# Spreading norms by whole-array transposes, padding the low parts to 128 rows, and shifting dense work into the pairs of a delta-rule layer

## The chip, the cores and the metric

The kernel runs on one core of one Trainium2 chip. The metric is the device time of one launch in microseconds (us). The engines are TensorE (PE, matmuls; its weight loads are listed as PEld), VectorE (DVE), ScalarE (ACT), GpSimd (POOL) and SyncE (SP, which here only issues DMAs).

## The reference

A trunk of two residual layers over 512 tokens of width 1024, in float32: a spatial-gating MLP, a gated convolutional feed-forward layer, an RWKV-7 time-mixing layer and a second feed-forward layer, each behind an RMS norm. All edits lie in the time-mixing layer (16 heads of width 64):

```python
xx = token_shift(h) - h
xr, xw, xk, xv, xa, xg = (h + xx * mu[i] for i in range(6))
r, k, v = xr @ w_r, xk @ w_k, xv @ w_v
w = -softplus(-(w0 + tanh(xw @ w1) @ w2)) - 0.5
a = sigmoid(a0 + (xa @ a1) @ a2)
g = sigmoid(xg @ g1) @ g2
kk = heads(k * k_k)
kk = kk * rsqrt(maximum(sum(kk * kk, -1), 1e-24))     # norm over the 64 of a head
k = k * (1 + (a - 1) * k_a)
decay = exp(-exp(heads(w)))
# S_t = S_{t-1} diag(decay_t) + (S_{t-1} (-kk_t)) (kk_t a_t)^T + v_t k_t^T ;  y_t = S_t r_t
y = group_norm(wkv7_scan(...)) * ln_w + ln_b + sum(r * k * r_k, -1) * v
out = (y * g) @ w_o
```

## The kernel before, in words

Activations are kept transposed, features on the 128 partitions and the 512 tokens along the free dimension, as eight tiles of 128 features. Each large product is made of three matmuls of fp32r operands (`mm3`): every float32 operand is split into a rounded high part and a low part, and high x high, high x low and low x high are added up in PSUM. A *dense step* below is the work between two yields of `dense_steps`: two of the eight contraction tiles, six matmuls 128x128 by 512.

The recurrence is computed in chunks of 64 tokens. `rwkv_first` makes the low-rank products `r.lr` and the receptance. `rwkv_main` then runs these generators against each other:

- `pairs()` is the main work of the first part. It goes over eight pairs of heads. `decay(p)` (three yields) applies the second factors of the two low-rank products (`l2`, two column blocks loaded at a time by `second_factors`), takes tanh, a running sum over tokens and exponentials, and computes the norm of each key over its head: squares (L884), sums by head with tokens on the partitions (L894, eight columns), a reciprocal (L897), and a spread of these reciprocals back to features by tokens (L902, eight matmuls with an identity into `u.q`, each of two instructions and 64 output rows). `operands(p)` multiplies them into the keys (L922). `products(p)` (three yields) forms the within-chunk products and stores them to DRAM for the scan.
- `projections()` is the *fill*: eight key tiles, eight value tiles, then the gate's product (`gates`) and the output projection (`project`). The mixed inputs of the values, `r.mix(3, k)`, one ACT and one DVE operation and a split into high and low parts, are issued while the last two key tiles are multiplied. High and low parts share two rings of ten buffers (`mxh`, `mxl`), eight of which hold the key inputs until then. `value(m)` centres a value tile (L839), stores it for the scan, and later adds the bonus of its pair (L854, L856). `gate_mix` makes the mixed inputs of the gate.
- `invert(g)` is the *side* work: the inverses of the triangular blocks of four pairs, 31 short dependent steps of two DVE operations and then small matmuls.
- `scan(g)` goes over the eight chunks of a group of four pairs in order, three yields each; `finish` normalises the result of every two chunks.

`weave(main, side, fill, rate, lag, side_rate)` interleaves them: after each yield of the main work, `rate` is added to a due count, and for each whole unit one step of the fill is issued; its PE instructions are queued behind a recent PE instruction of the main work. `RATES` holds the rates of six stages: pairs up to the fourth, pairs beside the first inverse, first scan (beside the second inverse), second scan, the scan's last normalisation, and the last pair. What is left of the fill comes after the second scan. Within these rules a planner orders each engine's instructions; the engines then run them in that order.

The low part of the second factors is one tile, `l2[2]`, whose lower 64 rows belong to the decay and whose upper 64 rows to the in-context rate; each matmul with it contracts 64 rows (L872).

Of the kernel before, what the change touches and what calls it, by code (L numbers as in the profile page):

```python
# [12 lines left out]
F32 = mybir.dt.float32  # L13
F32R = mybir.dt.float32r
AF = mybir.ActivationFunctionType
ALU = mybir.AluOpType
# [4 lines left out]
P = 128  # L21
D = 1024
KT = 8
T = 512
NF = 22
C = 64
# [3 lines left out]
GN_EPS = 64e-5  # L30
C1 = -0.5 * math.exp(-0.5)

RATES = ((1.9, 2), (1.9, 6, 2.2), (0.66, 2, 1.15), (0.72, 2), (2, 2), (1.2, 6, 2.2))
LEAD = 1
WB = 4
FIRST0, WAIT, STEPS = 1, 1, (2, 2, 2, 2, 2)
# [108 lines left out]
class Emit:  # L145
# [596 lines left out]
    def rwkv_main(self, r, ctx, gain):  # L742
        nc, tc, A = self.nc, self.tc, self.A
        V, S, G = nc.vector, nc.scalar, nc.gpsimd
        h0, h1 = slice(0, 64), slice(64, 128)
        H = (h0, h1)
# [4 lines left out]
        ep = ctx.enter_context(tc.tile_pool(name="pairs", bufs=1))  # L751

        def tile_(shape, tag, bufs):
            return ep.tile(shape, F32, tag=tag, bufs=bufs, name=self.uid(tag))

        def tmp(tag, bufs, w=W2):
            return tile_([P, w], tag, bufs)

        def c3(t):
            return t.rearrange("p (c t) -> p c t", t=C)  # L760

        def bc(t, n):
            return t.unsqueeze(2).to_broadcast([t.shape[0], t.shape[1], n])

        ks, used, done, vdone = {}, set(), set(), set()
        l2 = []
# [3 lines left out]
        def second_factors(p):  # L770

            w32 = self.l2w.pop()
            l2[:] = [ep.tile([P, 2 * P], F32R, tag=f"l2{i}", bufs=1, name=self.uid("l2")) for i in range(3)]
            for j in range(2):
                w = w32[:, 512 * j:512 * j + 2 * P]
                S.copy(l2[j], w)
                V.tensor_tensor(l2[2][H[j]], w[H[j]], l2[j][H[j]].bitcast(F32), ALU.subtract)
            if p + 2 < KT:
                self.load_l2(p + 2)


        def projections():

            load = Ahead([lambda n=n, m=m: self.parts(n, m) for n in PARTS for m in range(KT)])

            def key(m, a):
                while m >= NKEY and m - NKEY not in used:
                    yield
                ks[m] = tmp("key", NKEY, T)
                S.copy(ks[m], a)  # L790

            for m in range(KT - 2):
                a = self.acc("mm")
                yield from self.dense_steps(a, load.take(), r.xk)
                yield from key(m, a)
                yield

            ws = [load.take(), load.take(False)]
            accs = [self.acc("mm") for _ in range(2)]
            xv = []  # L800
            for k in range(KT):
                for j in range(2):
                    self.mm3(accs[j], self.wcols(ws[j], k * P, P), r.xk[k], k == 0, k == KT - 1)
                while len(xv) < min(k + 3, KT):
                    xv.append(r.mix(3, len(xv)))
                if k == 4:
                    load.fetch()
                yield
            for j in range(2):
                yield from key(KT - 2 + j, accs[j])  # L810
            late = iter(())
            for m in range(KT):
                a = self.acc("mm")
                w = load.take()
                if m == KT - 2:
                    ga["w"] = load_gate(0)
                for n, _ in enumerate(self.dense_steps(a, w, xv)):
                    yield
                    next(late, None)
                    if m == KT - 1 and n == 0:  # L820
                        gw[0] = gate_weights(ga["w"])
                        ga["parts"] = self.gate_parts()
                    if m == KT - 1 and len(gx) < 2:
                        gx.append(gate_mix(len(gx)))
                for _ in late:
                    yield
                v = ip.tile([P, T], F32, tag="v", bufs=1, name=self.uid("v"))
                S.copy(v, a)
                late = value(m, v)
            next(late)  # L830
            tail.append(late)
# [30 lines left out]
        def scratch(tag):  # L862
            return self.gp.tile([P, T], F32, tag=tag, bufs=2 if tag == "sq" else 1, name=self.uid(tag))

        def decay(p, u):

            k, w = ks[p], slice(p % 2 * P, (p % 2 + 1) * P)
            accs = [self.acc("e") for _ in range(2)]
            for j in range(2):
                nc.tensor.matmul(accs[j], l2[j][:, w], r.lr[j], start=True, stop=False)  # L870
            for j in range(2):
                nc.tensor.matmul(accs[j], l2[2][H[j], w], r.lr[j][H[j]], start=False, stop=True)  # L872
            if p % 2 == 1 and p + 1 < KT:
                second_factors(p + 1)
            th, u.ta = scratch("sq"), tmp("ta", 2, T)
            for j, x in enumerate((th, u.ta)):
                S.activation(x, accs[j], AF.Tanh, scale=0.5, bias=dq(j, p))
            u.kn = tmp("kn", 2, T)
            S.activation(u.kn, k, AF.Copy, scale=dq(2, p))
            V.tensor_scalar(th, th, 1.0, None, ALU.add)  # L880
            yield
            V.tensor_tensor_scan(th, self.c("smask", T), th, 0.0, ALU.mult, ALU.add)
            sq = scratch("sq")
            S.activation(sq, u.kn, AF.Square)  # L884
            u.gt = tile_([P, NCH, C + 1], "gt", 1)
            G.memset(u.gt[:, :, 0:1], 1.0)
            S.activation(u.gt[:, :, 1:], c3(th), AF.Exp, scale=C1)
            S.activation(gc[:, p], c3(th)[:, :, C - 1], AF.Exp, scale=C1)
            u.ei = scratch("rb")
            S.activation(u.ei, th, AF.Exp, scale=-C1)  # L890

            q = self.acc("e")
            for b in range(4):
                nc.tensor.matmul(q[:, 2 * b:2 * b + 2], sq[:, b * P:(b + 1) * P], self.c("blk2", 2), start=True, stop=True)  # L894
            n2 = tile_([P, 8], "n2", 2)
            V.tensor_scalar(n2, q[:, 0:8], 1e-24, None, ALU.max)
            V.reciprocal(n2, n2)  # L897
            yield
            u.q = self.acc("e")
            for b in range(4):  # L900
                for hd in range(2):
                    nc.tensor.matmul(u.q[H[hd], b * P:(b + 1) * P], n2[:, 2 * b + hd:2 * b + hd + 1].to_broadcast([P, C]),  # L902
                                     self.c("ident", P), start=True, stop=True)
            yield

        def operands(p, u):
# [152 lines left out]
        def gate_mix(k):  # L1059
            with ExitStack() as behind:  # L1060
                for eng in (mybir.EngineType.DVE, mybir.EngineType.Activation):
                    behind.enter_context(tc.issue_after(self.last(eng)))
                j, t = 5 * KT + k, scratch("sq")
                S.activation(t, self.hz[k][:, 0:T], AF.Copy, scale=self.p("mu", j))
                V.scalar_tensor_tensor(t, self.h[k], self.omu[:, j:j + 1], t, ALU.mult, ALU.add)
                return self.operand(t)
# [56 lines left out]
        def load_gate(g):  # L1123
            cols = slice(512 * g, 512 * g + 512)
            w32 = self.wp.tile([P, 1024], F32, tag="w32", bufs=2, name=self.uid("w32"))
            self.wq.dma_start(w32[:, 0:512], A["g2"][0:P, cols])
            self.wq.dma_start(w32[0:32, 512:], A["g2"][P:P + 32, cols])
            return w32

        def gate_weights(w32):  # L1130
            ws = ep.tile([P, 512], F32R, tag="gw", bufs=1, name=self.uid("gw"))
            self.stack(ws, w32[0:32, 512:], False)
            return (*self.split(ep, w32[:, 0:512], [P, 512], "gw", bufs=1), ws)
# [186 lines left out]
        main = pairs()  # L1320
        self.weave(until(main, lambda: 3 in done), None, fill, *RATES[0], ktiles=STEPS[0])
        inv = invert(0)
        for _ in take(inv, FIRST0):
            pass
        self.weave(until(main, lambda: KT - 2 in done), inv, fill, *RATES[1], ktiles=STEPS[1])
        load(0, 0)
        self.weave(main, inv, fill, *RATES[5], ktiles=STEPS[1])
        ahead = invert(1)
# [4 lines left out]
        ep = ctx.enter_context(tc.tile_pool(name="scan", bufs=1))  # L1333
        inv = ahead
        r.sg = [ep.tile([P, T], F32R, name=f"sg{i}") for i in range(3)]
        for _ in range(LEAD):
            next(fill, None)
        self.weave(scan(0), inv, fill, *RATES[2], ktiles=STEPS[2])
        for _ in inv:
            pass  # L1340
        self.weave(scan(1, left.pop()), None, fill, *RATES[3], ktiles=STEPS[3])
        self.weave(left.pop(), None, fill, *RATES[4], ktiles=STEPS[4])
        for _ in fill:
# [71 lines left out]
```

## Time and profile before

| | |
|---|---|
| three runs | 1256.67, 1258.59, 1263.21 us (median 1258.59) |
| profiled execution | 1258.64 us, of which 1256.8 us from its first to its last instruction |
| granted clock of PE, mean | 0.998 |
| spatial-gating layer | about 0 to 157 us of the span |
| first feed-forward layer | about 157 to 516 us |
| time mixing: first products | about 516 to 574 us |
| time mixing: pairs | about 574 to 731 us |
| time mixing: first and second scan | about 731 to 847 us |
| time mixing: rest of the projection | about 847 to 890 us |
| second feed-forward layer and output | about 890 to 1257 us |

A row of the timeline reads: start in us, duration in us, engine, line of the kernel, operation, written tile <- read tiles, shape, count. A shape such as 64*128 ahead of the operand's says how much of the array a matmul uses, rows by columns. Matmul durations overlap, because they are pipelined and their ends are modelled. A row of the busy-time view reads: stretch of the span, its length, then busy us and count of instructions of each engine, the clock that PE was granted, the mean share of time that the DMA engines were busy, and GB/s.

### The profile page before, as it was taken

Reading aid. Unit: us, or ns where it says so; the run is one execution under the profiler, and the core shown is the slowest. Engines: PE = TensorE matmul, PEld = TensorE weight load, DVE = VectorE, ACT = ScalarE, POOL = GpSimd, SP = SyncE. Lnnn points to the kernel's source line nnn. Section 1 sums busy time; section 2 is a strip of 40 time slices with the busy share of each in tenths; the row PEclk is TensorE's granted clock in tenths of the full one; section 3 lists DMA queues with packets and bytes.
Section 4 is the critical chain, followed back from the end, with each engine's and each line's share of the span. In section 5 each row is a group of like instructions: output and inputs, shape, how many; then the busy total and the mean of one; then the engine's idle time right before and its main releaser. Section 6 shows DMA issues by size and latency. Waiting matters only on the chain.

```text
span 1256.8 us, 19427 instructions
## 1 busy us (share of the span) xinstructions
PE 1238.0 (98%) x7543; PEld 1003.2 (80%) x7543; DVE 856.3 (68%) x1403; ACT 627.7 (50%) x1080; POOL 95.0 (8%) x117
## 2 busy tenths in 40 slices
PE   9999999999999999999999999899999999999997
PEld 6878888888888888877777777677888888888886
DVE  6466568888886454775798898775677787773233
ACT  6444446555554333475676657533544454442322
POOL 4100200000000010000000022322100000000000
PEclk9999999999999999999999999999999999999999
DMA  7332457777656775325777799784323332333332
GB/s 260 103 101 84 130 170 243 244 248 246 205 165 204 219 218 191 108 87 191 218 200 215 217 242 219 205 205 135 93 92 101 101 99 88 99 96 93 105 96 80
DMA packets 115452, 201.65 MB, mean 160 GB/s; under 512 B 21600, under 2 KB 53600, under 8 KB 115360
## 3 DMA queue, kind: packets, MB, share of 16 engines
q10 hardware_dynamic: 39104, 112.87, 29.7%
q1 hardware_dynamic: 76256, 87.54, 23.6%
q8 instruction: 59, 0.97, 0.3%
q14 instruction: 33, 0.27, 0.1%
HBM read 152.93 MB, written 47.45 MB: 159 GB/s over the span
## 4 chain that ended last, share of the span: by engine, by line
PE 86%; DVE 7%; issue 1%; POOL 1%; ACT 0%; DMA 0%; DVEq 0%; POOLq 0%; ACTq 0%
PE mm L320 9%; PE mm L322 9%; PE mm L321 9%; PE aux L320 6%; PE aux L322 6%; PE aux L321 6%; PE e L320 6%; PE e L321 6%; PE us L320 6%; PE e L322 6%; PE us L322 6%; PE us L321 6%; DVE tt L1022 1%; PE aux L945 1%; DVE pr L1021 1%
## 5 line engine op out<-in xcount | busy, mean ns | idle before, releaser
L236 ACT CAST w<-w 128x512 fp32r<-128x512 f32 x340 | 205.9, 611 | 349.1 <-PE aux L322 88.5
L237 DVE TENSOR_TENSOR w<-w,w 128x512 fp32r<-128x512 f32 x340 | 232.5, 686 | 181.4 <-ACT w L236 180.9
L320 PE MATMUL mm<-mxh,w 128*128 128x512 f32 x416 | 170.0, 409 | 0.2 <-ACT vt L844 0.2
L321 PE MATMUL mm<-mxl,w 128*128 128x512 f32 x416 | 164.3, 395 | 0.0
L322 PE MATMUL mm<-mxh,w 128*128 128x512 f32 x416 | 164.2, 395 | 0.0
L347 POOL TENSOR_TENSOR ss<-ss,sq 128x512 f32<-128x512 f32 x30 | 40.8, 1362 | 768.8 <-ACT sq L345 706.1
L320 PEld LDWEIGHTS mm<-mxh,w 128*128 128x128 f32 x416 | 78.2, 188 | 20.2 <-issue 3.3
L322 PEld LDWEIGHTS mm<-mxh,w 128*128 128x128 f32 x416 | 78.4, 188 | 16.7 <-issue 0.7
L321 PEld LDWEIGHTS mm<-mxl,w 128*128 128x128 f32 x416 | 78.4, 188 | 15.6 <-issue 1.3
L549 ACT ACTIVATE cv<-z,par 128x512 f32<-128x512 f32 x88 | 71.7, 816 | 33.5 <-DVE z L547 28.7
L320 PE MATMUL aux<-mxh,w 128*128 128x512 f32 x216 | 84.5, 391 | 0.0
L320 PE MATMUL us<-mxh,w 128*128 128x512 f32 x216 | 84.5, 391 | 0.0
L322 PE MATMUL aux<-mxh,w 128*128 128x512 f32 x216 | 84.2, 390 | 0.0
L321 PE MATMUL us<-mxl,w 128*128 128x512 f32 x216 | 84.1, 389 | 0.0
L321 PE MATMUL aux<-mxl,w 128*128 128x512 f32 x216 | 84.1, 389 | 0.0
L322 PE MATMUL us<-mxh,w 128*128 128x512 f32 x216 | 84.0, 389 | 0.0
L320 PE MATMUL e<-mxh,w 128*128 128x512 f32 x208 | 81.4, 391 | 0.0
L321 PE MATMUL e<-mxl,w 128*128 128x512 f32 x208 | 81.2, 390 | 0.0
L322 PE MATMUL e<-mxh,w 128*128 128x512 f32 x208 | 81.0, 389 | 0.0
L550 DVE SCALAR_TENSOR_TENSOR cv<-z,par,cv 128x512 f32<-128x512 f32 x88 | 66.0, 751 | 19.5 <-ACT cv L549 19.5
L551 DVE SCALAR_TENSOR_TENSOR cv<-z,par,cv 128x512 f32<-128x512 f32 x88 | 66.0, 751 | 2.9
L237 DVE TENSOR_TENSOR pwl<-pw,pwh 128x512 fp32r<-128x512 f32 (+1 forms) x51 | 34.8, 682 | 19.8 <-DMA wkd<-pwl 4.6
(1081 smaller groups left out, 2559.8 us busy)
## 6 DMA issues: line engine op xcount, KB each, us to landing
w<-in_wup ACTq DMA_DIRECT2D x88, 512.0 KB, 3.6
w<-in_wdn ACTq DMA_DIRECT2D x32, 512.0 KB, 3.6
st<-std SPq DMA_DIRECT2D x30, 320.0 KB, 6.8
w<-wkd ACTq DMA_DIRECT2D x16, 512.0 KB, 4.5
w<-wvd ACTq DMA_DIRECT2D x16, 512.0 KB, 5.5
w<-wod ACTq DMA_DIRECT2D x16, 512.0 KB, 4.2
w<-in_wdn ACTq DMA_DIRECT2D x16, 384.0 KB, 3.3
w<-in_wsu ACTq DMA_DIRECT2D x8, 512.0 KB, 3.8
```

Of the source, the lines that this page charges most:

```text
L236: nc.scalar.copy(hi[r, :n], src)
L237: (lo_eng or nc.vector).tensor_tensor(lo[r, :n], src, hi[r, :n].bitcast(F32), ALU.subtract)
L320: mm(acc, wh, xh, start=first, stop=False)
L321: mm(acc, wh, xl, start=False, stop=False)
L322: mm(acc, wl, xh, start=False, stop=last)
L347: nc.gpsimd.tensor_tensor(self.ss, self.ss, self.sq, ALU.add)
L549: nc.scalar.activation(c, z[:, 2:], AF.Identity, scale=cw(2, i), bias=self.p("conv_b", l * 44 + i))
L550: nc.vector.scalar_tensor_tensor(c, z[:, 1:T + 1], cw(1, i), c, ALU.mult, ALU.add)
L551: nc.vector.scalar_tensor_tensor(c, z[:, 0:T], cw(0, i), c, ALU.mult, ALU.add)
L945: nc.tensor.matmul(qs[hd][:, c - ch.start, :], bk[H[hd], c, C * hd:C * hd + P], ar[H[hd], c, :], start=True, stop=True)
L1021: V.tensor_tensor(q, a, b, ALU.mult)
L1022: V.tensor_tensor(tt[:, 0:nj, j + 1:32], tt[:, 0:nj, j + 1:32], q, ALU.add)
```

## The change

Four edits. The reciprocals of the norms are first copied by ACT into a 128x512 array in which each stands 64 times, and four whole-array transposes then take the place of the eight half-wide matmuls. The low part of the second factors becomes two tiles of 128 rows, one for each product, of which 64 rows are zeros set once; its matmuls contract all 128 rows. The first mixed value inputs are issued after keys 4 and 5, into the two free buffers of the rings, and the others follow the release of the key inputs. And four of the rates change.

```diff
-RATES = ((1.9, 2), (1.9, 6, 2.2), (0.66, 2, 1.15), (0.72, 2), (2, 2), (1.2, 6, 2.2))
+RATES = ((2.1, 2), (2.1, 6, 2.2), (0.55, 2, 1.15), (0.72, 2), (2, 2), (1.3, 6, 2.2))
...
         def second_factors(p):
             w32 = self.l2w.pop()
-            l2[:] = [ep.tile([P, 2 * P], F32R, tag=f"l2{i}", bufs=1, name=self.uid("l2")) for i in range(3)]
+            if not l2:
+                l2[:] = [ep.tile([P, 2 * P], F32R, name=self.uid("l2")) for _ in range(4)]
+                for j in range(2):
+                    G.memset(l2[2 + j][H[1 - j]].bitcast(F32), 0.0)
             for j in range(2):
                 w = w32[:, 512 * j:512 * j + 2 * P]
                 S.copy(l2[j], w)
-                V.tensor_tensor(l2[2][H[j]], w[H[j]], l2[j][H[j]].bitcast(F32), ALU.subtract)
+                V.tensor_tensor(l2[2 + j][H[j]], w[H[j]], l2[j][H[j]].bitcast(F32), ALU.subtract)
...
+            xv = []
+
+            def mixed(n):
+                while len(xv) < n:
+                    xv.append(r.mix(3, len(xv)))
+
             for m in range(KT - 2):
                 a = self.acc("mm")
                 yield from self.dense_steps(a, load.take(), r.xk)
                 yield from key(m, a)
+                if m >= KT - 4:
+                    mixed(m - KT + 5)
                 yield
 
             ws = [load.take(), load.take(False)]
             accs = [self.acc("mm") for _ in range(2)]
-            xv = []
             for k in range(KT):
                 for j in range(2):
                     self.mm3(accs[j], self.wcols(ws[j], k * P, P), r.xk[k], k == 0, k == KT - 1)
-                while len(xv) < min(k + 3, KT):
-                    xv.append(r.mix(3, len(xv)))
+                mixed((3, 3, 4, 5, 5, 6, 7, 8)[k])
...
             for j in range(2):
-                nc.tensor.matmul(accs[j], l2[2][H[j], w], r.lr[j][H[j]], start=False, stop=True)
+                nc.tensor.matmul(accs[j], l2[2 + j][:, w], r.lr[j], start=False, stop=True)
...
             V.reciprocal(n2, n2)
+            nb = scratch("sq").rearrange("p (b c) -> p b c", c=C)
+            S.copy(nb, bc(n2, C))
             yield
             u.q = self.acc("e")
             for b in range(4):
-                for hd in range(2):
-                    nc.tensor.matmul(u.q[H[hd], b * P:(b + 1) * P], n2[:, 2 * b + hd:2 * b + hd + 1].to_broadcast([P, C]),
-                                     self.c("ident", P), start=True, stop=True)
+                nc.tensor.transpose(u.q[:, b * P:(b + 1) * P], nb[:, 2 * b:2 * b + 2].rearrange("p h c -> p (h c)"),
+                                    self.c("ident", P))
```

## The prediction

> **What bounds the kernel now.** I read the page first, then busy time by stage, then the order of single instructions on TensorE (PE) inside the recurrent layer, where every edit lies.
>
> ```profile
> PE 1238.0 (98%) x7543; PEld 1003.2 (80%) x7543; DVE 856.3 (68%) x1403; ACT 627.7 (50%) x1080; POOL 95.0 (8%) x117
> ...
> PE 86%; DVE 7%; issue 1%; POOL 1%; ACT 0%; DMA 0%; DVEq 0%; POOLq 0%; ACTq 0%
> ```
>
> PE is busy 98% of the span and carries 86% of the chain that ended last, so time taken off PE is time off the kernel, unless another engine is full at that place. The stages of the recurrent layer show where one is:
>
> ```profile
> core 0: us, PE busy (x) PEld busy (x) DVE busy (x) ACT busy (x) POOL busy (x), PEclk, DMA share, GB/s
> 574.00:664.00 90.00, 90.00 (x687) 68.51 (x686) 69.53 (x122) 64.99 (x119) 0.67 (x6) 1.00 0.70 203
> 664.00:731.50 67.50, 66.82 (x670) 51.93 (x670) 59.16 (x131) 42.29 (x85) 3.16 (x7) 0.97 0.74 213
> 731.50:761.40 29.90, 29.09 (x393) 22.07 (x392) 28.73 (x71) 15.06 (x33) 7.40 (x11) 1.00 1.06 256
> 761.40:795.00 33.60, 31.09 (x621) 24.07 (x620) 25.31 (x47) 23.62 (x42) 9.50 (x11) 1.00 0.91 221
> 795.00:821.00 26.00, 21.88 (x329) 15.57 (x327) 19.10 (x41) 13.42 (x27) 7.27 (x8) 1.00 0.76 196
> 821.00:846.60 25.60, 25.57 (x369) 20.03 (x369) 17.15 (x39) 6.72 (x17) 7.31 (x8) 1.00 0.82 210
> 846.60:890.00 43.40, 42.49 (x226) 34.93 (x225) 25.59 (x47) 16.26 (x30) 9.62 (x11) 1.00 0.38 123
> ```
>
> In order: the pairs before the first inverse (front), the pairs beside it (middle), chunks 0 to 3 of the first scan, its chunks 4 to 7, the head and the rest of the second scan, and the tail of projections. PE is full in the front, the middle and the tail. VectorE (DVE) has room in the front (77%), little in the middle (88%), and is itself full in chunks 0 to 3 (28.73 of 29.90 us). In the head of the second scan PE idles 4.1 us: no dense work is left that doesn't wait for the first scan's norm.
>
> **The change, part by part.** The cost of an operation on PE is read from starts of neighbours, since ends are modelled.
>
> ```profile
> 574.10 0.63 PE L870 MATMUL e<-lr,l 128*128 128x512 f32 x2
> 574.65 0.50 PE L872 MATMUL e<-lr,l 64*128 64x512 f32 x2
> 575.09 0.50 PE L320 MATMUL mm<-mxh,w 128*128 128x512 f32 x1
> 575.42 0.39 PE L321 MATMUL mm<-mxl,w 128*128 128x512 f32 x1
> 575.65 0.39 PE L322 MATMUL mm<-mxh,w 128*128 128x512 f32 x1
> ...
> 581.11 0.39 PE L321 MATMUL mm<-mxl,w 128*128 128x512 f32 x1
> 581.43 1.09 PE L902 MATMUL e<-cst,n 128*64 128x128 f32 x16
> 582.46 0.50 PE L322 MATMUL mm<-mxh,w 128*128 128x512 f32 x1
> 582.79 0.39 PE L870 MATMUL e<-lr,l 128*128 128x512 f32 x1
> 583.11 0.50 PE L872 MATMUL e<-lr,l 64*128 64x512 f32 x1
> 583.54 0.50 PE L320 MATMUL mm<-mxh,w 128*128 128x512 f32 x1
> 583.88 0.39 PE L321 MATMUL mm<-mxl,w 128*128 128x512 f32 x1
> ```
>
> Two dense matmuls start 0.23 us apart (575.42, 575.65), so a dense step of six is 1.4 us.
>
> *Norms (L902).* From L321 at 581.11 to L870 at 582.79 pass 1.68 us, of which two ordinary places are 0.46: the sixteen instructions cost 1.22 us, 0.2 of it the wider gaps on both sides. Four whole-array transposes of the same kind exist in the scan:
>
> ```profile
> 790.21 0.63 PE L1267 MATMUL aux<-cst,y 128*128 128x128 f32 x4 [0.31 <-DVE y L1263]
> 790.59 0.48 PE L320 MATMUL mm<-mxh,w 128*128 128x512 f32 x1
> 790.90 0.39 PE L321 MATMUL mm<-mxl,w 128*128 128x512 f32 x1
> ```
>
> They take 0.69 less one place, 0.46, and at most 0.1 more on entry: 0.5. Saved 0.7 us a pair, 5.6 us over eight.
>
> *Low parts (L872).* In pair 0 the two stand together: 574.10 to 575.42 is 1.32 us where five places of 0.23 would be 1.14, so 0.2 is saved. Where they stand alone, as at 583.11, 582.79 to 583.88 is 1.09 against 0.69: 0.4 each. The order on PE has them alone in pairs 1 and 2 and together in the other six: 4 x 0.4 + 6 x 0.2 = 2.8 us. PE is thus relieved of 8.4 us in all. The operands' added rows are zeros set once on POOL before the first pair; the copies and subtractions on ScalarE (ACT) and DVE keep their sizes.
>
> The Trainium skill, "TensorEngine Tiling (Array Packing)", Key Properties, says that changing the tiling mode drains TensorE; the gaps of 0.32 and 0.43 us around L872 agree. Its Performance Considerations advise row tiling for a contraction of 64 or less, which speaks against this edit; the two of pair 0 do fall in one 0.44 us place, and the drains cost more than that wins.
>
> *The copy of the spread norms.* New on ACT, eight times 128x512, and a wait: it needs the reciprocal from DVE, with later activations queued behind it, and the transposes, then the product with the keys on DVE (L922), wait for it.
>
> ```profile
> 622.18 0.62 ACT L929 COPY bk<-bk 64x512 f32<-64x512 f32 x1 [1.00 <-DVE bk L924]
> ...
> 683.07 0.20 DVE L897 RECIPROCAL n<-n 128x8 f32<-128x8 f32 x1
> 686.41 1.09 PE L902 MATMUL e<-cst,n 128*64 128x128 f32 x16
> 687.55 0.69 DVE L922 TENSOR_TENSOR kn<-kn,e 128x512 f32<-128x512 f32 x1 [1.64 <-PE e L902]
> 691.36 0.53 ACTq L247 DMA_DIRECT2D w<-wvd  x1
> ```
>
> 0.62 us each, 5 us on ACT, which is busy 107 of 157 us over the pairs. At 683 PE reaches the spread 3.1 us after the reciprocal, so the copy lies inside PE's queue and I take 0. If that cover were gone each would cost its 0.62 on PE, 5 us in all. The lower end is 0 too: an added copy starts nothing sooner.
>
> *Rates.* The weave adds the rate at each of the main work's steps and gives out whole fill steps. Counting yields in the code: 19, 9 and 2 main steps of the pairs gave 36, 17 and 2 fill steps and will give 39, 18 and 2; the first scan's 24 gave 15 and will give 13, of which the last is no longer dense. Dense steps: front 35 to 38, middle 21 to 22, first scan 15 to 12, second scan 11 to 12, the weave after it 10 and 10, tail 44 to 42. With them the value columns' other work moves by about one column: centring (L839) into the front, bonus (L854 on PE, L856 on DVE) into the middle, each out of the scan, and the column's load, two issues of 0.53 us on ACT's queue, and its store on SP's. The DMA engines are at 1.06 in chunks 0 to 3 and 0.70 to 0.74 in the pairs, so these move to where there is room.
>
> ```profile
> L839 PE MATMUL mm<-cst,v 128*128 128x128 f32 x64 | 10.4, 299 | 0.1
> L854 PE MATMUL mm<-rt,wb 128*128 128x512 f32 x16 | 8.6, 618 | 0.0
> ...
> L237 DVE TENSOR_TENSOR mxl<-sq,mxh 128x512 fp32r<-128x512 f32 x8 | 6.7, 832 | 0.4 <-ACT mxh L236 0.4
> L1065 DVE SCALAR_TENSOR_TENSOR sq<-h,omu,sq 128x512 f32<-128x512 f32 x8 | 5.9, 744 | 0.5 <-ACT sq L1064 0.5
> L856 DVE TENSOR_TENSOR rt<-mm,v 128x512 f32<-128x512 f32 x7 | 4.8, 688 | 0.9 <-PE mm L854 0.8
> ```
>
> An eighth of the first two is 1.3 and 1.1 us; neighbours overlap, so I take 1.0 for each.
>
> *First value inputs.* The same eight mixes, the first two issued beside keys 4 and 5 and the others a little later than now: nothing is added, and in the front DVE has 20 us to spare. Taken at 0; from 0 to 1.4 us gained, the two DVE operations of one mix (0.74 and 0.69 us by the rows for the gate's mixes and for L856).
>
> **The sum.** Front, PE full: six spreads 4.2 and low parts 2.6 off, three steps 4.1 and a centring 1.0 on: -1.7. Middle, PE full: two spreads and one pair's low parts 1.6 off, a step 1.4 and a bonus 1.0 on: +0.8. First scan, chunks 0 to 3: the yields put four of the gate's mixes there instead of two and one more bonus: 2 x 1.57 + 0.69 = 3.8 us on a DVE that is full; 32.5 at the present 96% is 33.9 us: +4.0. Chunks 4 to 7: two steps, a centring and two bonuses leave a PE busy 31.09 of 33.60: -5.7. A chunk of the second scan takes 6 us where little dense work stands in it, so four have a floor of 24 and 27.9 is possible.
>
> ```profile
> 823.62 0.69 PE L1214 MATMUL us<-vu,st 128*64 128x64 f32 x16
> 829.67 0.69 PE L1214 MATMUL us<-vu,st 128*64 128x64 f32 x16
> ```
>
> Second scan: one more dense step, in the head's 4.1 us of idle PE: 0. Tail: two steps fewer: -2.7. Sum: -1.7 + 0.8 + 4.0 - 5.7 - 2.7 = -5.3 us. The profiled execution took 1258.64 us (span 1256.8 and 1.8 around it), 0.05 from the median of the three runs, 1258.59. Forecast: 1253.3 us. What is late next is DVE in the first chunks of the scan.
>
> **The rivals.** *All of PE's saving arrives*: DVE takes the mixes where it waits for PE anyway. For it: PE sets 86% of the chain; against it: the 96% of DVE in chunks 0 to 3. 1258.6 - 8.4 = 1250.2.
>
> There is a bonus to it. PE ran at a lower clock once:
>
> ```profile
> 680.50:684.50 4.00, 4.00 (x15) 3.39 (x14) 3.96 (x10) 2.16 (x6) 0.00 (x0) 0.58 0.67 204
> ```
>
> 0.58 over 4 us is 1.7 us lost, just after a run of small matmuls. With another mix of work there it may go, 1248.5, or come twice. The Trainium skill, "TensorE: Matmul & The Clock Gate", Part 1, ties the half clock to an activity window with little in it; that the trace shows PE occupied here means occupancy alone does not keep the clock up.
>
> *DVE sets the pairs and the first scan*: the 221 us from 574 to 795 stay as long as they are, with DVE at 88% and 96% in their middle, and only the tail's 2.7 us go: 1255.9. Against it: the front, where DVE is at 77%.
>
> *Slower*: the copy is late. ACT is in order; if the copy stands behind other activations, or they behind it while it waits for the reciprocal, kn, the products, and the next pair come late. With x us on the path in each of eight pairs the time is 1253.3 + 8x; it passes 1264.9 (slower by 0.5%) at x = 1.45. With 2 us it is 1269.3. For it: DVE waited 1.64 us for L902 at 687; against it: 3.1 us of cover there.
>
> *The low parts lose*: if the two row tiles of 64 ran side by side without draining, a pair would be one place and padding would add 0.23 x 8 = 1.8 instead of saving 2.8: 1253.3 + 4.6 = 1257.9. The rows show the drains, so 3 in 100. The Trainium skill's advice on small contractions ("TensorEngine Tiling (Array Packing)", Performance Considerations) would come out so.
>
> **How the numbers follow.** Half a per cent, 6.3 us, is about what a measurement of this kernel tells from no change: faster is below 1252.3, slower above 1264.9. Chances: the forecast 0.37, all of PE's saving 0.32, DVE 0.19, low parts 0.03, late copy 0.09. Of the forecast's share a third falls below 1252.3 (mixes placed better, the clock): faster 0.44. Slower 0.09, the rest 0.47. The range runs from 1248.0, the full saving with the clock, to 1259.5, the DVE case with its copies uncovered by half (2.5 us) and the mixing of chunks dearer by a microsecond.
>
> **What would show it.** L902 as four whole-array transposes a pair at about 0.5 us; no gap of 0.4 us after the second-factor matmuls; 60 dense steps before the scan instead of 56; the first scan shorter mainly in its last four chunks, with DVE above 95% in the first four; a projection tail shorter by two steps. Wrong would be: PE waiting for ACT at the transposes, idle time on PE in the middle above its present 0.7 us, or a first scan as long as before.

## The result, and the profile after

The changed kernel took 1283.18 us (median of four runs, 1276.88 to 1284.58) against 1259.73 us of the kernel before beside it: 1.0178 times as long, interval 1.0158 to 1.0199. The prediction was 1253.3 us, its range 1248.0 to 1259.5; the change is 23 us slower. The profiled execution took 1284.58 us, with a span of 1282.8 against 1256.8.

The page of the changed kernel: busy time of PE, the granted clock in 40 slices, the chain that ended last.

```profile
PE 1255.0 (98%) x7447; PEld 1021.3 (80%) x7447; DVE 855.8 (67%) x1403; ACT 630.9 (49%) x1088; POOL 94.7 (7%) x119
PEclk9999999999999999999998989799999999999999
PE 86%; DVE 6%; issue 2%; ACT 1%; POOL 0%; DMA 0%; DVEq 0%; POOLq 0%; ACTq 0%; SPq 0%
```

PE is still busy 98% and carries 86% of the chain, with 96 instructions fewer and 17 us more of busy time. The clock row differs most: it has slices under 9 in the recurrent layer, where the kernel before has none:

```profile
PEclk9999999999999999999999999999999999999999
```

Busy time by stage of the changed kernel (stretch, length, busy us of PE, PEld, DVE, ACT and POOL with counts, PEclk, DMA share, GB/s): two rows for the pairs, chunks 0 to 3 and 4 to 7 of the first scan, the second scan, the tail.

```profile
574.00:664.00 90.00, 88.45 (x584) 71.33 (x584) 65.92 (x116) 62.80 (x119) 0.69 (x6) 0.98 0.71 205
664.00:748.80 84.80, 83.20 (x722) 65.67 (x720) 64.31 (x140) 52.40 (x101) 3.44 (x9) 0.90 0.73 196
748.80:781.30 32.50, 28.97 (x387) 21.45 (x386) 26.70 (x62) 15.10 (x34) 6.29 (x8) 0.95 0.91 227
781.30:818.50 37.20, 32.11 (x582) 24.75 (x582) 24.26 (x53) 19.77 (x35) 9.01 (x12) 0.77 0.65 166
818.50:873.00 54.50, 50.08 (x689) 38.26 (x685) 36.98 (x81) 19.27 (x44) 14.86 (x16) 0.94 0.71 192
873.00:914.00 41.00, 39.59 (x237) 32.36 (x237) 24.98 (x46) 16.23 (x30) 9.64 (x11) 1.00 0.36 115
```

The second scan took 50.5 us before:

```profile
795.00:845.50 50.50, 46.34 (x667) 34.57 (x665) 35.60 (x79) 20.14 (x44) 14.58 (x16) 1.00 0.79 200
```

The pairs grew from 157.5 to 174.8 us, chunks 0 to 3 from 29.9 to 32.5, chunks 4 to 7 from 33.6 to 37.2, the second scan by 4.0; the tail fell by about 2 (the layer's last addition ends at 886.4 us before and at 912.0 after). Of the pairs' 17.3 us, 2.0 lie ahead of them: their first product started at 574.10 us before, and now starts at

```profile
576.08 0.62 PE L879 MATMUL e<-lr,l 128*128 128x512 f32 x2
```

after a stretch at half clock that the changed kernel's profile has at 21 us and that of the kernel before has not. Before, PE's clock was below 1.00 in one of these stages, now in all but the tail.

Read finer, in steps of 3.4 us set by the clock record, the changed kernel shows what lies behind a lower mean clock:

```profile
645.30:648.70 3.40, 3.12 (x50) 2.76 (x48) 3.37 (x7) 3.35 (x8) 0.00 (x0) 1.00 1.10 362
648.70:652.10 3.40, 2.26 (x16) 2.00 (x16) 3.37 (x7) 3.40 (x7) 0.00 (x0) 1.00 0.36 101
652.10:655.50 3.40, 3.40 (x9) 2.72 (x9) 3.40 (x8) 2.44 (x7) 0.00 (x0) 0.50 0.65 173
...
792.10:795.50 3.40, 1.90 (x68) 1.59 (x68) 3.40 (x7) 0.82 (x1) 0.00 (x0) 1.00 0.30 82
795.50:798.90 3.40, 1.86 (x34) 1.43 (x34) 1.82 (x4) 3.30 (x6) 0.00 (x0) 0.50 0.00 0
798.90:802.30 3.40, 3.40 (x65) 2.80 (x64) 0.84 (x2) 3.27 (x7) 0.64 (x3) 0.50 0.02 5
```

The clock is 1.00 or 0.50 and changes only at the edge of such a window. In the window before each of these two drops DVE is full (3.37 and 3.40 us) and PE short of work (2.26 and 1.90 us). The clock drops six times in the layer. DVE is full before four of the drops; it has room in the window before the one at 764.8 (2.33 us), and before the one at 826.2 (2.03). Before the one at 734.0 PE is listed as busy throughout:

```profile
730.60:734.00 3.40, 3.40 (x58) 2.88 (x57) 3.33 (x5) 2.64 (x4) 0.00 (x0) 1.00 0.68 196
761.40:764.80 3.40, 0.80 (x15) 0.47 (x16) 2.33 (x4) 2.91 (x6) 0.68 (x1) 1.00 1.01 259
```

PE's order around the first drop in the changed kernel (start, us, line, tiles, shape, count, and the wait ahead of it):

```profile
649.84 0.93 PE L955 MATMUL aux<-ar,bk 64*128 64x128 f32 x6 [1.42 <-DVE lq L959]
650.70 1.05 PE L903 MATMUL e<-cst,sq 128*128 128x2 f32 x8
651.69 0.48 PE L955 MATMUL aux<-ar,bk 64*128 64x128 f32 x2
652.10 0.80 PE L320 MATMUL mm<-mxh,w 128*128 128x512 f32 x1
652.70 0.63 PE L321 MATMUL mm<-mxl,w 128*128 128x512 f32 x1
653.12 0.63 PE L322 MATMUL mm<-mxh,w 128*128 128x512 f32 x1
```

From 648.7 PE runs only small matmuls and waits 1.42 us for DVE; then the dense ones come 0.42 us apart (652.70, 653.12) instead of 0.23. The profile of the kernel before has one drop, also behind a full DVE, with PE listed as busy 3.26 us of the 3.40:

```profile
677.80:681.20 3.40, 3.26 (x31) 2.86 (x31) 3.40 (x9) 2.05 (x5) 0.00 (x0) 1.00 0.50 159
681.20:684.60 3.40, 3.40 (x13) 2.92 (x12) 3.37 (x10) 1.49 (x4) 0.00 (x0) 0.50 0.80 243
```

The clock records count, up to the end of the last matmuls, 3.4 us at half clock before and 51.2 after (once at 21 us, the rest from 652 to 833 us). Half of the difference, (51.2 - 3.4) / 2 = 23.9 us, is about what it cost if PE had work throughout; the spans differ by 26.0. These are two single executions. Of 51 other executions of the kernel before, beside the experiments, the mean clock was 0.993 to 0.998, and that of its profile was 0.998. One minus the mean clock, times the span, is on average 25.0 us in the four executions of the changed kernel and 5.5 us in those 51: 19.5 us, where the mean spans differ by 22.7.

### The profile page after: what moved, and what is told of

Same layout as the page of the kernel before. It is cut to its first block, busy times and chain, and to the rows that moved or that the text cites. A ratio compares the mean times of both kernels' runs of the same rounds, so it can differ in the third digit from the quotient of the medians.

```text
span 1282.8 us, 19256 instructions
## 1 busy us (share of the span) xinstructions
PE 1255.0 (98%) x7447; PEld 1021.3 (80%) x7447; DVE 855.8 (67%) x1403; ACT 630.9 (49%) x1088; POOL 94.7 (7%) x119
## 4 chain that ended last, share of the span: by engine, by line
PE 86%; DVE 6%; issue 2%; ACT 1%; POOL 0%; DMA 0%; DVEq 0%; POOLq 0%; ACTq 0%; SPq 0%
PE mm L320 9%; PE mm L321 9%; PE mm L322 8%; PE aux L320 6%; PE aux L322 6%; PE aux L321 6%; PE e L320 6%; PE e L321 6%; PE e L322 6%; PE us L320 6%; PE us L322 5%; PE us L321 5%; PE aux L955 1%; DVE pr L1031 1%; DVE tt L1032 1%
## 5 line engine op out<-in xcount | busy, mean ns | idle before, releaser
L320 PE MATMUL mm<-mxh,w 128*128 128x512 f32 x416 | 170.9, 412 | 2.8 <-ACT mxh L236 2.8
L321 PE MATMUL mm<-mxl,w 128*128 128x512 f32 x416 | 167.0, 401 | 0.0
L322 PE MATMUL mm<-mxh,w 128*128 128x512 f32 x416 | 167.0, 401 | 0.0
L320 PEld LDWEIGHTS mm<-mxh,w 128*128 128x128 f32 x416 | 79.7, 192 | 20.7 <-ACT mxh L236 3.1
L322 PEld LDWEIGHTS mm<-mxh,w 128*128 128x128 f32 x416 | 79.9, 192 | 17.3 <-issue 0.5
L550 DVE SCALAR_TENSOR_TENSOR cv<-z,par,cv 128x512 f32<-128x512 f32 x88 | 66.0, 752 | 19.5 <-ACT cv L549 19.4
```

The source lines that it names most:

```text
L320: mm(acc, wh, xh, start=first, stop=False)
L321: mm(acc, wh, xl, start=False, stop=False)
L322: mm(acc, wl, xh, start=False, stop=last)
L550: nc.vector.scalar_tensor_tensor(c, z[:, 1:T + 1], cw(1, i), c, ALU.mult, ALU.add)
```

## The experiments

The table has every kernel that ran: its median, that of the kernel before in the same batch, and from the profiled execution the span and the us at half clock ahead of the last matmuls.

| kernel | median | before | span | half clock |
|---|---|---|---|---|
| the changed kernel | 1283.18 | 1259.73 | 1282.8 | 51.2 |
| a_rates: changed, old rates | 1268.87 | 1258.4 | 1265.3 | 13.7 |
| a_mix: changed, old place of the mixes | 1283.81 | 1258.4 | 1286.1 | 61.4 |
| a_norm: changed, old norms | 1272.2 | 1258.4 | 1267.2 | 27.3 |
| a_low: changed, old low parts | 1284.57 | 1258.4 | 1287.1 | 58.0 |
| b_rates: before, new rates | 1277.02 | 1258.51 | 1276.1 | 37.5 |
| b_norm: before, new norms | 1279.82 | 1258.51 | 1277.6 | 37.5 |
| b_copy: before, the copy alone | 1269.12 | 1258.51 | 1267.4 | 13.6 |
| b_both: before, new norms and the old matmuls too | 1273.46 | 1258.51 | 1273.3 | 13.7 |
| b_dve: before, transposes, array made on DVE | 1281.89 | 1258.9 | 1280.1 | 34.1 |
| w_before: before, heavy dose | 1294.21 | 1258.9 | 1292.0 | 3.4 |
| w_rates: new rates, heavy dose | 1292.42 | 1258.9 | 1289.7 | 0 |
| w_all: changed, heavy dose | 1290.35 | 1258.9 | 1288.6 | 6.8 |
| w_norm: new norms, heavy dose | 1292.19 | 1258.27 | 1290.6 | 3.4 |
| w_lowmix: low parts and mixes, heavy dose | 1293.35 | 1258.27 | 1291.3 | 6.8 |
| v_one: changed, light dose | 1275.24 | 1258.27 | 1273.7 | 34.1 |
| v_two: changed, double light dose | 1273.24 | 1258.27 | 1268.5 | 13.7 |
| b_lowmix: before, low parts and mixes | 1256.83 | 1259.28 | 1256.3 | 6.8 |
| b_low: before, low parts | 1255.42 | 1259.28 | 1253.8 | 3.4 |

**One edit undone at a time.** Each takes one part of the diff shown above out of the changed kernel. The theories put the loss down to the rates (R), the copy and transposes (N) or the later mixes (M).

```diff
 # a_rates
-RATES = ((2.1, 2), (2.1, 6, 2.2), (0.55, 2, 1.15), (0.72, 2), (2, 2), (1.3, 6, 2.2))
+RATES = ((1.9, 2), (1.9, 6, 2.2), (0.66, 2, 1.15), (0.72, 2), (2, 2), (1.2, 6, 2.2))
 # a_mix:  mixes issued as before;  a_norm: L902 as before, no copy;  a_low: l2[2] of 64 rows as before
```

> The changed kernel with the rates of before; the other three edits stay. Theory R (the rates: dense work runs ahead of the value inputs in the pairs, the first scan is thinned, and PE's clock is halved in both): all of the loss goes, 1250 to 1258 us, mean clock back to 0.99 or more. Theory N (the copy and the transposes delay the pairs or count as little work for PE's clock): most of the loss stays, 1275 to 1285 us, clock below 0.985. Theory M (the later mixes starve the values): most stays as well, 1270 to 1285 us.

> The changed kernel with the mixed value inputs issued as before (all beside the last two keys, three ahead); the new rates, transposes and padding stay. Theory M: 1255 to 1262 us. Theory R: little changes, 1275 to 1285 us. Theory N: the same 1275 to 1285 us.

> The changed kernel with the norms spread by the eight half-wide matmuls of before, without the copy; the other three edits stay. Theory N: 1255 to 1262 us, clock back to 0.99. Theory R: 1278 to 1290 us, since 5.6 us of PE work come back. Theory M: the same.

> The changed kernel with the low parts as one tile contracted over 64 rows as before; the other three edits stay. All three theories: 1280 to 1290 us (2.8 us of PE work come back). If padding is what costs: 1255 to 1262 us.

Ratios to the kernel before: 1.0083 (1.0059 to 1.0106) with the old rates, 1.0101 (1.0078 to 1.0123) with the old norms, 1.0194 (1.0149 to 1.0238) with the old mixes, 1.0203 (1.016 to 1.0247) with the old low parts. So undoing the mixes or the low parts takes nothing off that can be told apart, and neither the rates nor the norms are needed for the loss: without either one, some 10 to 13 us of it stay. No theory had put down such a time for these two runs, since each gave the loss mainly to one edit. The half clock goes with the span: (13.7 - 3.4) / 2 = 5.2 of +8.5 us of span, and in the same order 12.0 of +10.4, 29.0 of +29.3 and 27.3 of +30.3.

**One edit added at a time, and the norms edit in parts.** Theory C: transposes do little for PE's clock. Theory D: the copy comes late.

```diff
 # b_copy: the copy as in the change; the old eight matmuls read it
-                    nc.tensor.matmul(u.q[H[hd], b * P:(b + 1) * P], n2[:, 2 * b + hd:2 * b + hd + 1].to_broadcast([P, C]),
+                    nc.tensor.matmul(u.q[H[hd], b * P:(b + 1) * P], nb[:, 2 * b + hd],
                     ...
 # b_both: the old eight matmuls from n2 run ahead of the four transposes, into the same place
 # b_dve: the four transposes as in the change, no copy on ACT
-            V.reciprocal(n2, n2)
+            nb = scratch("sq").rearrange("p (b c) -> p b c", c=C)
+            V.reciprocal(nb, bc(n2, C))
```

> The kernel before with the new rates alone. Removing them from the changed kernel took 14.3 us off. If rates and norms add up: 1270 to 1274 us, with 20 to 30 us of the span at half clock. If the rates hurt only beside the transposes: 1256 to 1262 us, clock 0.99 or more.

> The kernel before with the norms' edit alone (copy and transposes). If it costs on its own: 1266 to 1272 us. If only together with the new rates: 1250 to 1256 us, its 5.6 us of PE work gained.

> The kernel before, with ACT's copy of the spread reciprocals, read by the eight half-wide matmuls of before instead of by transposes: the wait and the ACT time of the edit, with PE's work as before. Theory D (the copy comes late and holds up the pairs): as slow as the norms' edit alone, 1264 to 1272 us. Theory C (the transposes count as little work for PE's clock, and the copy is covered): 1257 to 1261 us, clock 0.99 or more.

> The kernel before with the norms' edit, but the eight half-wide matmuls of before are issued as well, into the same bank, just ahead of the transposes that overwrite them: 1.2 us more PE work a pair than the edit alone. Theory C: faster than the edit alone or equal to it, since the clock stays up; 1260 to 1264 us. Theory D: slower than the edit alone by up to 10 us.

> From the kernel before: the four whole-array transposes, but no copy on ACT: DVE's reciprocal reads each of its eight columns 64 times and writes the 128x512 array itself. Theory W (what the norms edit loses, 21 us alone, is the wait for ACT's copy that stands in an in-order queue): most of it goes, 1252 to 1264 us. Theory C (whole-array transposes in the place of half-wide matmuls let the clock drop): 1272 us or more with over 25 us at half clock. In either case DVE takes eight longer reciprocals, by the 128x512 rows about 0.5 us each, 4 us on an engine that is 77 to 88% busy there.

The rates alone cost 18.5 us (1.0128, 1.0099 to 1.0156), the norms alone 21.3 (1.0164, 1.0147 to 1.018), all four edits together 23 to 25: losses that are no sum, and each of the two is above the ranges put down for it. Of the rates' +19.3 us of span, half clock accounts for (37.5 - 3.4) / 2 = 17.1, and they add no instruction. Of the norms' +20.8 it accounts for as much; the other 3.7 stand where 5.6 were to be saved, so some 9 us of that edit are not the clock. b_both is told best by comparison: it has the eight old matmuls to do on top of the norms edit, 1.2 us a pair by the prediction's row, and is 6.4 us faster than b_norm, at 13.7 us of half clock instead of 37.5. Of its +16.5 us of span the clock accounts for 5.2 and the old matmuls, at 1.2 a pair, for 9.6; its time is above the 1260 to 1264 us put down for C. That it is faster speaks for C; but the old matmuls also stream 16 x 128 columns a pair where the transposes stream 4 x 128, so that it does not show that a transpose counts for less than another matmul of its size.

The copy alone costs 10.6 us (1.0084, 1.006 to 1.0109), of which half clock explains (13.6 - 3.4) / 2 = 5.1. That is in the range put down for D, but the norms edit, which D has as slow as the copy, took 10.7 us more. That DVE waits longer for the spread is in the trace of the changed kernel too, which waits 10.3 us at its eight products with the keys:

```profile
L932 DVE TENSOR_TENSOR kn<-kn,e 128x512 f32<-128x512 f32 x8 | 5.5, 686 | 10.3 <-PE e L912 10.3
```

and in that of the kernel before, 2.5 us:

```profile
L922 DVE TENSOR_TENSOR kn<-kn,e 128x512 f32<-128x512 f32 x8 | 5.5, 683 | 2.5 <-PE e L902 2.5
```

So D holds for a part. b_dve, meant to tell C from D (there called W), tells nothing, though its time and its 34.1 us of half clock lie where C had them: its reciprocal took much longer than I had counted, 26.8 us of DVE, so neither theory was tested by it.

```profile
L898 DVE RECIPROCAL sq<-n 128x512 f32<-128x512 f32 x8 | 26.8, 3350 | 0.2
```

**The clock held up by idle matmuls.** Theory P: a stretch of 3.4 us in which few columns stream is followed by one at half clock, and that is what makes the changed kernel slow. Theory Q: the moved work leaves PE waiting, and the clock only follows. Products of two constants, overwritten at once, go on PE where it is short of work, into the bank that the next small matmuls write.

```diff
+    def heat(self, q, n):
+        for _ in range(n):
+            self.nc.tensor.matmul(q, self.c("ident", P), self.c("smask", T)[:, 0:q.shape[-1]], start=True, stop=True)
 # pairs 4 to 7: heat(the us bank, 2) ahead of each of the three product steps
 # chunks 3 to 7 of the first scan, chunk 0 of the second: heat(us, 2), heat(us[:, 1], 2), heat(us[:, 0], 2)
 #   ahead of the first products, of those with ti, and of those with bt
```

> The kernel before with idle matmuls put on PE, whose results are overwritten: a 128x512 product of two constants, twice, into the us bank ahead of each of the three product steps of pairs 4 to 7, and in chunks 3 to 7 of the first scan and chunk 0 of the second two of 512 columns ahead of the chunk's first products and two of 256 columns ahead of each of its next two. By the cadence of 0.23 us that is 10.9 us of added PE work. This is the control: the kernel before had 3.4 us at half clock outside its end, so nothing is to be won. Theory P (the slowdown is PE's clock: a stretch of 3.4 us in which few columns stream is followed by one at half clock): 1259 to 1271 us, 0 to 12 slower, at no more than 7 us of half clock. Theory Q (the moved work leaves PE waiting, the clock only follows): the same.

> The same idle matmuls in the kernel with the new rates alone, which took 18.5 us more than the kernel before and had 34 us more at half clock (17 us lost). Theory P: half clock falls below 20 us, the time stands within 7 us of the control with the old rates, and below the 1277.0 us without the idle matmuls although PE has 10.9 us more to do. Theory Q: still 15 to 20 us above the control, about 1280 to 1290 us.

> The same idle matmuls in the changed kernel (1283.2 us, 51 us at half clock outside its end). Theory P: half clock falls below 25 us, the time to between 1262 and 1276 us, faster than the changed kernel although PE has 10.9 us more to do. Theory Q: 24 us above the control as before, 1283 to 1296 us.

The dose was far heavier than planned: in the control, w_before, it is 46.5 us of PE, since a fp32 product of 512 columns runs as two instructions (which the profile counts one by one):

```profile
L1360 PE MATMUL us<-cst 128*128 128x512 f32 (+1 forms) x116 | 46.5, 519 | 1.2 <-ACT vu L1239 1.1
```

The control took 35 us more than the kernel before (1.0274, 1.0253 to 1.0296). The times put down, which counted on 10.9 us of dose, are therefore missed: theory P had the new rates below 1277.0 us and all four edits at 1262 to 1276. Only the comparison with the control is left. The clock is nearly full in all three (3.4, 0 and 6.8 us at half), and with that the loss is gone: 1292.42 us with the new rates and 1290.35 with all four edits (1.0247, 1.0218 to 1.0276), where without the dose they stood 18.5 and 23 us above. Theory Q wanted 15 to 24 us above the control; both stand below it, though by no more than the intervals. The objection remains that so heavy a dose covers waits. So next a cheap dose on the changed kernel, and the other edits with the heavy one.

```diff
 # v_one, v_two: bf16, one pass; n is 1 and 2
-            self.nc.tensor.matmul(q, self.c("ident", P), self.c("smask", T)[:, 0:q.shape[-1]], start=True, stop=True)
+            self.nc.tensor.matmul(q, self.c("ident", C).bitcast(mybir.dt.bfloat16),
+                                  self.c("smask", q.shape[-1] // 2).bitcast(mybir.dt.bfloat16), start=True, stop=True)
```

> The changed kernel with a light dose of idle matmuls: bf16, of one pass (by the dense cadence 0.23 us for 512 columns), one at each of the same places, 5.5 us of added PE work in all and none of it used. Theory P (the clock): half clock falls below 40 us from 51, and the time below the changed kernel's 1283.2 us in spite of the added work, 1268 to 1281. Theory Q (waits; the clock only follows): 1283 to 1290 us.

> The same with two at each place, 11 us of added PE work. Theory P: half clock below 25 us, 1264 to 1279 us. Theory Q: 1285 to 1296 us.

> The norms edit alone with the heavy dose (the control of the old code took 1294.2 us with it, at a clock of 0.997). Without the dose the norms edit alone cost 21 us. Theory P: with the clock held up the edit gives what the prediction counted for it, 5.6 us off, less what the copy on ACT costs: 1286 to 1293 us, at under 10 us of half clock. Theory W (ACT's copy comes late and PE or DVE waits for it, whatever the clock): 1300 us or more.

> The low parts and the earlier mixes, at the old rates and with the old norms, with the heavy dose. Theory P: 2.8 us off for the low parts, nothing for the mixes: 1289 to 1294 us against the control's 1294.2. Theory Q: within 2 us of the control or above it.

Both light doses came out as theory P had put down. Adding unused work made the changed kernel faster: 1275.24 us with one idle matmul at each place (1.0132 times the kernel before, 1.0117 to 1.0148, against 1.0178, 1.0158 to 1.0199, without) and 1273.24 with two (1.0127, 1.0105 to 1.0149). Half clock fell from 51.2 to 34.1 and 13.7 us. In v_one the dose is

```profile
L1370 PE MATMUL us<-cst 128*128 128x512 bf16 (+1 forms) x23 | 8.0, 348 | 3.1 <-ACT vu L1249 1.8 <-DVE wt L1236 1.3
```

A wait, or any of the queues, cannot become shorter through more work in PE's order except by way of the clock or of another order; the planner did choose another order in each of these kernels, which is a reserve here. Executions of one and the same program, whose order is the same, speak to it. The four of the changed kernel had spans of 1282.8, 1282.7, 1280.1 and 1275.1 us at mean clocks of 0.979, 0.978, 0.980 and 0.985. From the first to the last the clock rose by 0.006, which over some 1280 us is 7.7 us, and the span fell by 7.7. In a_low the step from 0.975 to 0.985 is 12.8 us by the clock, and the spans differ by 9.5 (1287.1 and 1277.6). Why one execution of a program has more windows at half clock than another is not shown.

With the heavy dose the norms edit comes to 1.0272 times the kernel before (1.0254 to 1.029) and the low parts with the mixes to 1.0276 (1.0261 to 1.0291). Both are in theory P's ranges (the second in theory Q's as well) and within the control's interval, at 3.4 and 6.8 us of half clock: the loss of the norms edit is gone, and a gain of it, or of the low parts, can't be told from none.

**The edits that take least off PE.**

> From the kernel before: the low parts over 128 rows and the earlier mixes; the old rates and the old spread of the norms, no idle matmuls. These are the two edits that remove least PE work, so they are the version that could be the fastest. Prediction's terms (clock as before): 2.8 us off, 1254 to 1258 us. Theory P: those hold only if no more windows fall under half clock than the one of before; each window more costs 1.7 us: with three to six more 1260 to 1266 us.

> The low parts alone. Prediction's term: 2.8 us off, 1254 to 1258 us. Theory P: the same plus 1.7 us for each window of 3.4 us at half clock beyond the one of before; two to four of them, 1258 to 1265 us, because the edit takes PE work out of stretches that are already poor in it.

The low parts alone are faster than both kernels: 0.9974 (0.9957 to 0.9991), 3.3 us off in twelve runs; with the mixes 0.9979 (0.9968 to 0.9991). The profile of b_low has no half clock in the recurrent layer, but one window at 21 us, so that the total is that of the kernel before. From its first product with `l2` (574.10 us before, 575.9 here) to its last addition (886.4 and 883.3) the layer takes 4.9 us less; 1.7 of that is the window that went, 3.2 is left. With the mixes, two windows fall in the second scan:

```profile
807.60:811.10 3.50, 1.96 (x36) 1.33 (x36) 2.65 (x7) 0.37 (x1) 0.00 (x0) 1.00 0.81 181
811.10:814.50 3.40, 2.65 (x48) 2.49 (x48) 2.43 (x6) 1.35 (x3) 3.08 (x3) 0.50 0.29 78
814.50:817.90 3.40, 3.40 (x22) 2.44 (x20) 2.40 (x7) 0.83 (x2) 0.09 (x1) 0.50 0.88 214
```

Here the layer takes 310.9 us instead of 312.3, and without its one window more it would take 3.1 less than before. Theory P had put down two to six windows more for these two runs: none more came in b_low and one more in b_lowmix, and both times lie in the 1254 to 1258 us of the prediction's term.

**What decides a window.** From 27 to 1245 us the traces of all 20 kernels hold 7,120 windows of 3.413 us. For each I added up the columns that PE's matmuls stream, each weighted with the rows that it uses out of 128 (64 rows count half). Of 108 windows with under 2,060 such columns 84 were followed by half clock, of the other 7,012 only 31; the limit of 2,060 was chosen to fit these same records. Dense work at 0.23 us for 512 columns streams 7,600 in a window. So it is a count of streamed work, not time listed as busy, that went with the clock: the window of the kernel before at 677.8 has PE busy 3.26 of 3.40 us, mostly with products over 64 rows. That the count is columns by rows is a fit and not shown; counting the transposes as nothing fits as well.

The Trainium skill, "TensorE: Matmul & The Clock Gate", Part 1, has two clock states and a free-running window of 3413 ns; the records here agree, 1.00 or 0.50, in multiples of 3.41 us. The Trainium skill, on that page in "Why this matters for your kernels", advises against idle gaps of PE of more than about 3 us. Here the clock fell without such a gap: the longest wait in the window before the drop at 652.1 was 1.42 us.

## Why the prediction was wrong, point by point

*The step that failed* is the one on the clock. The prediction saw the one half-clock window, priced it rightly at 1.7 us, put it just after a run of small matmuls, and then took it as a bonus that "may go, or come twice". It came fourteen times in the layer, and once at 21 us. The row that the prediction read, with PE busy 4.00 us of 4.00, is mostly the window at half clock itself; what leads to it stands in the window before, where mostly small products ran. The rule put first, "time taken off PE is time off the kernel, unless another engine is full at that place", lacked that case: where PE waits for another engine, mostly a full DVE, work taken off PE leaves a window with too little in it, and the dense work behind it then runs at half speed. Each such window costs up to 1.7 us; a spread was to save 0.7.

*Stages.* I take half of its half-clock time off each stage (20.4 us in the pairs against 3.4 before, 20.5 in the first scan, 6.8 in the second), and the 2.0 us ahead of the pairs. The differences are then: pairs +17.3 - 2.0 - 8.5 = +6.8 where -0.9 was forecast; first scan +6.2 - 10.2 = -4.0 (forecast -1.7); second scan +4.0 - 3.4 = +0.6 (0); tail -2.0 (-2.7). That is +1.4 in all where -5.3 was forecast, so 6.7 us of the miss are not the clock. The second scan and the tail were near, and the pairs were not. In the first scan only the total is near. Chunks 0 to 3 came to 32.5 us where 33.9 was forecast, but that is luck: DVE, which was to be full there, was busy 26.70 us of 32.50, with four mixes as counted but one bonus where three were counted, and fewer steps of the inverse; without the clock they would have taken 30.8. Chunks 4 to 7 came to 37.2, and to 28.7 without the clock, where 27.9 was forecast: taking two dense steps out of them made PE poorest exactly there (clock 0.77).

*Pairs.* The groups of dense matmuls ahead of the first scan, in the kernel before:

```profile
L320 PE MATMUL mm<-mxh,w 128*128 128x512 f32 x104 | 45.7, 440 | 0.0
L322 PE MATMUL mm<-mxh,w 128*128 128x512 f32 x105 | 42.4, 404 | 0.0
L321 PE MATMUL mm<-mxl,w 128*128 128x512 f32 x105 | 42.4, 403 | 0.0
```

and in the changed kernel:

```profile
L320 PE MATMUL mm<-mxh,w 128*128 128x512 f32 x115 | 49.9, 434 | 0.0
L322 PE MATMUL mm<-mxh,w 128*128 128x512 f32 x116 | 48.0, 414 | 0.0
L321 PE MATMUL mm<-mxl,w 128*128 128x512 f32 x115 | 47.4, 412 | 0.0
```

are 314 and 346, 32 more. Eight of these ran in the 2.0 us ahead of the pairs; from 576.0 us on there are 338, so 24 more, the four steps of the forecast. PE's idle time there rose from 0.7 to 3.1 us, against the prediction's 0.7. The other 5.3 of the 7.7 us between +6.8 and -0.9 I could not place. They are about what the copy alone cost beyond its half clock (below), but that they are the same is not shown.

*Norms.* The transposes cost what was said:

```profile
658.38 0.39 PE L322 MATMUL mm<-mxh,w 128*128 128x512 f32 x1
658.62 0.60 PE L912 MATMUL e<-cst,sq 128*128 128x128 f32 x4
658.97 0.47 PE L320 MATMUL mm<-mxh,w 128*128 128x512 f32 x1
659.28 0.39 PE L321 MATMUL mm<-mxl,w 128*128 128x512 f32 x1
```

658.38 to 659.28 is 0.90 us less two places of 0.23: 0.44 (forecast 0.5). But the 5.6 us saved did not reach the end: with the clock held up nothing that can be told from none, and a loss of 21 without.

*The copy* was taken at 0, with 5 us in all as its upper end. Alone it cost 10.6 us, some 5.5 of it beyond the half clock: even so a little above the upper end. The cover of 3.1 us that the prediction read at 683 stood for one pair only: in the other seven the spread starts 0.2 to 2.2 us after the reciprocal.

*Low parts*: 2.8 us forecast, 3.3 measured alone (1.1 to 5.4 by its interval). Without the clock the layer is 3.2 us shorter in the profile of b_low and 3.1 in that of b_lowmix, so this term and its reason hold.

*Mixes* at 0: nothing in the time that can be told apart.

*Rates*: the dense steps left the first scan about as counted, and the new rates by themselves cost 18.5 us. Of the ten windows that b_rates has at half clock in the layer, five follow each other from 789.0 to 806.0 us, in the last chunks of the first scan, which had given dense steps up.

*The rivals.* None happened. The one that ended slower, the late copy, named a cost that exists but not the one that decided. The clock should have stood there as the rival on the other side, with its place (chunks 4 to 7 and the last pairs, where PE waits for DVE), its price (1.7 us a window) and its point of decision: with 5.3 us to be saved, a fourth window more makes a loss of it.

## What to carry to other kernels

Where PE waits for another engine, work taken off it can save nothing and cost the clock: count the columns that stream in each 3.4 us before thinning such a stretch out, above all by moving dense work away. When a small edit has a large effect, look at the granted clock by stage first and at the instructions second. Cheap unused matmuls are a good test for it: if a kernel becomes faster with more work, look to the clock, and compare executions of one program, whose order is the same, to be surer; here the idle matmuls did not win as much as leaving the thinning out.

## What was not expected of the hardware

PE can be listed busy for 3.26 of 3.40 us and still be put at half clock in the next window, when the work is mostly products over 64 rows and of two columns. A fp32 product of 128x512 from constants took two instructions of 0.46 us each, four times the 0.23 us of the dense ones:

```profile
735.46 1.88 PE L1370 MATMUL us<-cst 128*128 128x512 f32 x4
737.27 0.37 PE L959 MATMUL aux<-ar,bk 64*128 64x128 f32 x1
```

(w_all: two products as four instructions, 1.81 us to the next start). And a reciprocal of 512 elements a partition took 3.35 us on DVE against 0.20 us for eight.
